# Weight differences of the second half: buffers of their own, stores one weight tile later, loads pinned behind weight loads

## The chip, the cores and the metric

The kernel runs on one core of one Trainium2 chip. The metric is the device time in microseconds (us) of one execution; lower is better. The core has TensorE (PE, matrix products), VectorE (DVE), ScalarE (ACT), GpSimd (POOL) and SyncE (SP). SP does no arithmetic here: it issues the transfers (DMAs) one after the other, in the order in which they stand in its queue. A transfer whose condition isn't met yet holds up all that stand behind it in that queue.

## The reference

One decoder block (DEPTH 1) on 512 tokens of 2048 channels in f32, with sixteen heads of 64 channels in attention and eight groups of 128 channels in spatial gating:

```python
mod = silu(c) @ w_ada + b_ada                       # shift, scale, gate
h = rms_norm(x, norm_g) * (1 + scale) + shift
z = h @ w_in                                        # 2048 -> 7184
u_a, v_a, g_a, q_b, k_b, v_b, g_b, f_b = split(z)
y_a = chunked_spatial_gating(gelu(u_a), gelu(v_a), ln_g, ln_b, w_s, b_s) * silu(g_a)
y_b = forgetting_attention(q_b, k_b, v_b, f_b, b_f) * silu(g_b)
y = concatenate([y_a, y_b]) @ w_out                 # 2048 -> 2048
out = rms_norm(x + gate * y, final_g)
```

forgetting_attention is causal softmax attention whose logits get the difference of two cumulated sums of log(sigmoid(f)) added. Group A mixes the tokens of each chunk of 128 by a lower triangular 128 x 128 matrix per group.

## The kernel before

**Products.** Every f32 operand is split into a rounded high part and the rest, its low part. A product is then three PE products: high by high, low by high, high by low (lines 145 to 147 in mm_cols, where weights are stationary; 154 to 156 in mm_toks, where the tokens are).

**Weight tiles.** w_tile (L117) brings a weight tile in: SP loads 512 KB (one weight tile) into a raw tile of the pool tag "raw" with four buffers (L123), ScalarE makes whi from it (L129), and VectorE (in some groups POOL) subtracts to make wlo (L130). A raw buffer is free again when that subtraction is done. The instructions of w_tile have a raised priority (WPRI), so a planner, which orders the instructions of each engine ahead of time by its own estimated timeline, puts them well ahead of the products that use them: the loads stand about four weight tiles ahead.

**Work between the tiles.** After the products of each weight tile the code calls tick(), which takes one entry from a list `slots` and one from a list `fillers`. `slots` holds the attention of the four groups of heads (u = 0 to 3), in eight entries each: scores, the softmax sums (lse), probabilities (probs) and values. `fillers` holds work that is independent of the products. The projection's column groups come in the order va, ga, v0, q0, k0, gb0, q1, k1, v1, gb2, q2, k2, v2, q3, k3, v3, gb1, gb3. The output projection follows, in two halves of 1024 columns: unit(0) and unit(1).

**The softmax sums.** lse takes the sums of a group of four heads, turns them with a PE transpose, splits them into a tile lt, and eight small DMAs on SP (L507) copy rows of lt into the tiles that hold q (the rows "q<-lt" of a profile). Only then can PE make the products t of probs (L523 and L524; the second reads those rows). After these come exponentials, splits, and the products of values.

**The weight differences.** The output projection makes each half with seven block products in place of eight. Four of the seven need differences of blocks of w_out: b12 - b11, b12 - b22, b22 - b11 and b21 - b22. They are made in advance and stored in DRAM (tsum, "ts" in the profile). For the first half this is done in eight steps (sum_step) while va is made. For the second half it is done in sixteen parts (sum_part, k = 0 to 7, p = 0 and 1; in the text part number 2k + p, counted from 0, in the profile ts_k_p). Each part is one filler: two loads of 256 KB (L640, L641) into a [128, 4, 256] tile of the tag "raw", the same four buffers as the weight tiles; four subtractions on POOL (L644); one store of 512 KB (L646). The store stands in SP's queue where the planner puts it, and whatever stands behind it waits until POOL's last subtraction is done.

**The gate.** The same list has 32 gate_steps, in which POOL builds the adaLN gate (L603, L604) from 512 KB loads in "raw", and four gate_sums. Before the change the order of the list is: gate_steps of all four column groups with gate_sum(0) to gate_sum(2) among them, then parts 0 to 2, gate_sum(3), and parts 3 to 15.

**wsp.** A [128, 8, 2, 128] tile holds the split matrices of spatial gating (8 KB per partition). It is last read by mix_head, early in the projection. Its pool buffer is used again by a tile "wide" in unit(1) alone.

Of the kernel before, what the change touches and what calls it, by code (L numbers as in the profile page):

```python
# [8 lines left out]
F32 = mybir.dt.float32  # L9
F32R = mybir.dt.float32r  # L10
# [5 lines left out]
P = 128  # L16
# [11 lines left out]
def trunk_kernel(  # L28
# [70 lines left out]
    newest = [None]  # L99
    newest_mm = [None]  # L100

    def load(dst, src, late=False):
        with ExitStack() as es:
            if queue:
                es.enter_context(tc.issue_after((newest[0] if late else queue[-1]).ins))
            newest[0] = nc.sync.dma_start(dst, src)
            if CHAIN[0]:
                queue.append(newest[0])

    hh = [None] * KB  # L110
# [6 lines left out]
    def w_tile(segs, k0, nk, src=win_r, name="", pri=WPRI, loeng=None):  # L117
        n = sum(w for _, w in segs)
        with tc.high_priority(offset=pri):
            raw = wp.tile([P, nk, n], F32, tag="raw", name=f"raw_{name}", bufs=4)  # L120
            o = 0
            for c0, w in segs:
                (load if pri == 0 else nc.sync.dma_start)(  # L123
                    raw[:, :, o : o + w], src[:, k0 : k0 + nk, c0 : c0 + w]
                )
                o += w
            hi = wp.tile([P, nk, n], F32R, tag="whi", name=f"whi_{name}")
            lo = wp.tile([P, nk, n], F32R, tag="wlo", name=f"wlo_{name}")
            nc.scalar.activation(hi, raw, AF.Copy)  # L129
            (loeng or nc.vector).tensor_tensor(lo, raw, hi.bitcast(F32), ALU.subtract)  # L130
        return hi, lo
# [294 lines left out]
    vs_ = []  # L426
    wsp = pb.tile([P, 8, 2, P], F32R, name="wsp", tag="wsp")
    OFF = [0, 512, 896, 1152]
# [184 lines left out]
    def sum_step(u, k):  # L613
# [18 lines left out]
        else:  # L632
            nc.sync.dma_start(tsum[u][k // 2][:, :, js], o)

    def sum_part(u, k, p):

        c = slice(p * 256, p * 256 + 256)
        a = wp.tile([P, 4, 256], F32, tag="raw", name=f"ts{u}_{k}_{p}", bufs=4)
        w = wout_r[:, :, u * 1024 : (u + 1) * 1024].rearrange("p k (s n) -> p k s n", s=2)
        nc.sync.dma_start(a[:, 0:2, :], w[:, 8 + k, :, c])  # L640
        nc.sync.dma_start(a[:, 2:4, :], w[:, k, :, c])  # L641
        b11, b12, b21, b22 = (a[:, z, :] for z in range(4))
        for dst, l, r in ((b11, b12, b11), (b12, b12, b22), (b22, b22, b11), (b21, b21, b22)):
            nc.gpsimd.tensor_tensor(dst, l, r, ALU.subtract)  # L644
        o = (k % 2) * 512 + p * 256
        nc.sync.dma_start(tsum[u][k // 2][:, :, o : o + 256], a)  # L646

# [11 lines left out]
    def spatial_weights():  # L659
# [10 lines left out]
        for i in range(2):  # L670
            wt = bank("x", f"wsT{i}")
            for j in range(4):
# [3 lines left out]
            split(  # L676
                wsp[:, 4 * i : 4 * i + 4, 0, :], wsp[:, 4 * i : 4 * i + 4, 1, :],
                wt32.rearrange("p (h t) -> p h t", t=P),
# [80 lines left out]
    def mix_head(h):  # L759
# [4 lines left out]
        b2 = bias2[:, h, :]  # L764
        w2 = wsp[:, h].rearrange("p a t -> p (a t)")
        for n in range(2):
# [31 lines left out]
    v_group(0)  # L798
    heads_tiles()
    for g in range(4):  # L800
        for i in range(8):
            fillers.append(lambda g=g, i=i: gate_step(g, i))
            if g and i == 2:
                fillers.append(lambda g=g: gate_sum(g - 1))
    parts = [lambda k=k, p=p: sum_part(1, k, p) for k in range(8) for p in range(2)]
    fillers.extend(parts[:3] + [lambda: gate_sum(3)] + parts[3:])
    qk_group(0)
# [155 lines left out]
    def unit(u):  # L963
# [35 lines left out]
        if u:  # L999
            wide = pb.tile([P, 4, 512], F32, name="wide", tag="wsp")  # L1000
            u2, u3 = [wide[:, t, :] for t in range(2)], [wide[:, 2 + t, :] for t in range(2)]
        else:
            u2, u3 = tiles("u2", "yb", 8), tiles("u3", "yb", 8)
# [124 lines left out]
```

## Time and profile before

| what | before |
|---|---|
| median of 3 runs | 913.16 us (911.5 to 913.87) |
| profiled execution, its own time | 910.78 us |
| span of the profiled execution | 909.1 us |
| granted TensorE clock, mean | 0.988 |
| PE busy | 880.1 us (97%) |
| VectorE, ScalarE, POOL busy | 603.9, 445.4, 405.9 us |
| DMA | 188.91 MB, 208 GB/s |
| POOL's subtractions of the parts (L644) | 64, 53.3 us busy |
| POOL's gate steps (L603, L604) | 60 + 60, 195.7 us busy |

A row of the profile names line, engine, operation and tiles as out<-in, then the time it was busy, and in brackets how long the engine stood idle ahead of it and what ended that. The span is divided into 40 slices, each digit the busy tenths of one. Durations and places come from the one profiled execution, whose own time is 910.78 us; the three timed runs lie between 911.5 and 913.87 us.

### The profile page before, as it was taken

To read this page: it belongs to the slowest core of one execution; us is meant where nothing else is said; L and a number is where in the kernel's file an instruction comes from. 1 tells how busy PE (TensorE), PEld (TensorE's weight loads), DVE (VectorE), ACT (ScalarE), POOL (GpSimd) and SP (SyncE) were. 2 spreads that over 40 slices of the span, in tenths; PEclk is the share of its full clock that TensorE was granted. 3 is DMA by queue.
4 is the path that set the end of the run, shared out by engine and by line. 5 is a ranking of instruction groups with operands and counts; after the bars stand their busy time and mean duration, and the time that the engine had idled before them with its cause. 6 is when DMAs were issued, how large, how long until landed. Compare 5 with 4: busy or idle time off the path is not lost.

```text
span 909.1 us, 12698 instructions
## 1 busy us (share of the span) xinstructions
PE 880.1 (97%) x4408; PEld 744.3 (82%) x4408; DVE 603.9 (66%) x998; ACT 445.4 (49%) x775; POOL 405.9 (45%) x322
## 2 busy tenths in 40 slices
PE   6999999999999999999999999989999999999995
PEld 4888888887878997777889888978898888888884
DVE  4778888374547857454886554535655679996687
ACT  5663323452313234455666544645556657655454
POOL 1356554513324259888988879334641000000001
PEclk8999999999999999999999999999999999999999
DMA  9999996349893264545545454657686236577575
GB/s 339 353 352 355 355 318 202 110 147 323 305 332 110 51 190 140 154 144 156 170 129 163 152 148 155 201 182 220 208 246 203 76 104 220 186 242 250 180 238 202
DMA packets 139713, 188.91 MB, mean 208 GB/s; under 512 B 9968, under 2 KB 103360, under 8 KB 139136
## 3 DMA queue, kind: packets, MB, share of 16 engines
q1 hardware_dynamic: 139216, 187.53, 64.6%
q8 instruction: 35, 0.57, 0.3%
q10 hardware_dynamic: 432, 0.57, 0.2%
q14 instruction: 30, 0.25, 0.1%
HBM read 166.90 MB, written 20.97 MB: 207 GB/s over the span
## 4 chain that ended last, share of the span: by engine, by line
PE 77%; DMA 10%; DVE 5%; POOL 3%; issue 2%; ACT 2%; SPq 0%; POOLq 0%; ACTq 0%; DVEq 0%
PE s L145 6%; PE s L147 6%; PE s L146 6%; PE va L156 3%; PE va L155 3%; PE va L154 3%; PE gb L145 3%; PE gb L146 3%; PE gb L147 3%; PE vb L154 3%; PE vb L156 3%; PE vb L155 3%; PE k L147 2%; PE k L146 2%; PE woZ L911 2%
## 5 line engine op out<-in xcount | busy, mean ns | idle before, releaser
L603 POOL TENSOR_SCALAR gate<-gate,sc 128x512 f32<-128x512 f32 x60 | 103.7, 1738 | 24.5 <-DMA gate<-in_w_ada_dram 11.9
L604 POOL TENSOR_TENSOR gate<-gate,gate 128x512 f32<-128x512 f32 x60 | 92.0, 1536 | 1.7
L130 POOL TENSOR_TENSOR wlo_st<-raw_st,whi_st 128x1024 fp32r<-128x1024 f32 (+3 forms) x36 | 68.4, 1904 | 54.1 <-ACT whi_st L129 52.9
L145 PE MATMUL s<-hh,whi_st 128*128 128x512 f32 x224 | 87.8, 395 | 1.5 <-ACT hh L267 1.5
L146 PE MATMUL s<-hl,whi_st 128*128 128x512 f32 x224 | 87.8, 392 | 0.0
L66 ACT ACTIVATE whi_p<-p 128x1024 fp32r<-128x1024 f32 x52 | 55.2, 1061 | 55.2 <-PE woZ L912 20.1
L644 POOL TENSOR_TENSOR ts<-ts 128x256 f32<-128x256 f32 x64 | 53.3, 837 | 62.8 <-DMA ts<-in_w_out_dram 43.8
L244 DVE SCALAR_TENSOR_TENSOR acc<-ada,sc,acc 128x512 f32<-128x512 f32 x98 | 73.9, 754 | 6.7 <-DMA ada<-in_w_ada_dram 4.0
L67 DVE TENSOR_TENSOR wlo_p<-p,whi_p 128x1024 fp32r<-128x1024 f32 x52 | 63.4, 1220 | 20.2 <-ACT whi_p L66 20.1
L147 PE MATMUL s<-hh,wlo_st 128*128 128x512 f32 x224 | 76.1, 393 | 0.0
L155 PE MATMUL vb<-whi_vb,hl 128*128 128x256 f32 (+1 forms) x256 | 72.6, 286 | 0.0
L154 PE MATMUL vb<-whi_vb,hh 128*128 128x256 f32 (+1 forms) x256 | 71.8, 284 | 0.0
L156 PE MATMUL vb<-wlo_vb,hh 128*128 128x256 f32 (+1 forms) x256 | 71.1, 286 | 0.0
L129 ACT ACTIVATE whi_st<-raw_st 128x1024 fp32r<-128x1024 f32 (+3 forms) x36 | 31.2, 870 | 66.7 <-PE s L146 38.8
L955 POOL TENSOR_TENSOR sfin<-sfin,nhalf 128x1 f32<-128x1 f32 x2 | 1.5, 749 | 137.4 <-DVE sfin L1047 137.4
L145 PE MATMUL q<-hh,whi_q 128*128 128x512 f32 x128 | 51.4, 401 | 1.2 <-ACT whi_q L129 1.2
L146 PE MATMUL q<-hl,whi_q 128*128 128x512 f32 x128 | 51.0, 398 | 0.0
L145 PE MATMUL gb<-hh,whi_gb 128*128 128x512 f32 x128 | 50.4, 393 | 0.5 <-ACT whi_gb L129 0.5
L145 PEld LDWEIGHTS s<-hh,whi_st 128*128 128x128 f32 x224 | 42.4, 190 | 10.3 <-ACT hh L267 1.6
L145 PE MATMUL k<-hh,whi_k 128*128 128x512 f32 x128 | 50.0, 391 | 0.7 <-ACT whi_k L129 0.7
L154 PE MATMUL va<-whi_va,hh 128*128 128x512 f32 x128 | 50.3, 393 | 0.0
L147 PE MATMUL q<-hh,wlo_q 128*128 128x512 f32 x128 | 50.2, 399 | 0.1
(309 smaller groups left out, 2506.3 us busy)
## 6 DMA issues: line engine op xcount, KB each, us to landing
ada<-in_w_ada_dram SPq DMA_DIRECT2D x128, 256.0 KB
gate<-in_w_ada_dram SPq DMA_DIRECT2D x32, 512.0 KB
p<-ts SPq DMA_DIRECT2D x32, 512.0 KB
p<-in_w_out_dram SPq DMA_DIRECT2D x24, 512.0 KB
raw_va<-in_w_in_dram SPq DMA_DIRECT2D x16, 512.0 KB
raw_q<-in_w_in_dram SPq DMA_DIRECT2D x16, 512.0 KB
raw_k<-in_w_in_dram SPq DMA_DIRECT2D x16, 512.0 KB
raw_gb<-in_w_in_dram SPq DMA_DIRECT2D x16, 512.0 KB
```

The source lines that it names most:

```text
L66: a = nc.scalar.activation(hi, src, AF.Copy)
L67: return a, (eng or nc.vector).tensor_tensor(lo, src, hi.bitcast(F32), ALU.subtract)
L130: (loeng or nc.vector).tensor_tensor(lo, raw, hi.bitcast(F32), ALU.subtract)
L145: nc.tensor.matmul(pt, hi[:, j, cs], hh[k], start=(k == first), stop=False)
L146: nc.tensor.matmul(pt, hi[:, j, cs], hl[k], start=False, stop=False)
L147: nc.tensor.matmul(pt, lo[:, j, cs], hh[k], start=False, stop=(k == last))
L154: nc.tensor.matmul(o, ah[k][:, tsl], hi[:, j, :], start=(k == first), stop=False)
L155: nc.tensor.matmul(o, al[k][:, tsl], hi[:, j, :], start=False, stop=False)
L156: nc.tensor.matmul(o, ah[k][:, tsl], lo[:, j, :], start=False, stop=(k == last))
L244: nc.vector.scalar_tensor_tensor(sb if kk == KB - 1 else a, ga[:, j], col, a, ALU.mult, ALU.add)
L603: nc.gpsimd.tensor_scalar(ga[:, j], ga[:, j], sc[:, kk : kk + 1], None, ALU.mult)
L604: nc.gpsimd.tensor_tensor(a, a, ga[:, j], ALU.add)
```

## The change

1. Parts take their buffers from the tag "wsp", with two buffers of 4 KB per partition, and no longer from "raw". So that the tag fits, wsp becomes two tiles (heads 0 to 3 and 4 to 7) and "wide" becomes two tiles.
2. The loads of a part are pinned (tc.issue_after) behind the newest weight load that has been issued when sum_part runs: the planner may not put them ahead of it.
3. The store of a part is no longer issued in sum_part. It is kept as a function in late_stores and issued at the start of the next sum_part, one filler and so one weight tile later; it is pinned behind the newest weight load of that time. A last filler issues the store of part 15.
4. The order of the fillers: all gate work first, then two empty entries, gate_sum(3), and the 16 parts.

Lines after L105 are moved by the change: L123 is L125 after it, L145 to L147 become L147 to L149, L507 is L509, L524 is L526, L640 and L641 are both L648, L646 is L656.

```diff
--- before.py
+++ after.py
@@ -98,6 +98,7 @@
 
     newest = [None]
     newest_mm = [None]
+    newest_w = [None]
 
     def load(dst, src, late=False):
         with ExitStack() as es:
@@ -106,6 +107,7 @@
             newest[0] = nc.sync.dma_start(dst, src)
             if CHAIN[0]:
                 queue.append(newest[0])
+        return newest[0]
 
     hh = [None] * KB
     hl = [None] * KB
@@ -120,7 +122,7 @@
             raw = wp.tile([P, nk, n], F32, tag="raw", name=f"raw_{name}", bufs=4)
             o = 0
             for c0, w in segs:
-                (load if pri == 0 else nc.sync.dma_start)(
+                newest_w[0] = (load if pri == 0 else nc.sync.dma_start)(
                     raw[:, :, o : o + w], src[:, k0 : k0 + nk, c0 : c0 + w]
                 )
                 o += w
@@ -424,7 +426,7 @@
 
     fsplit = pb.tile([16, 2, S], F32R, name="fsplit", tag="fs")
     vs_ = []
-    wsp = pb.tile([P, 8, 2, P], F32R, name="wsp", tag="wsp")
+    wsp = [pb.tile([P, 4, 2, P], F32R, name=f"wsp{i}", tag="wsp", bufs=2) for i in range(2)]
     OFF = [0, 512, 896, 1152]
     sgb = {}
 
@@ -632,18 +634,28 @@
         else:
             nc.sync.dma_start(tsum[u][k // 2][:, :, js], o)
 
+    late_stores = []
+
     def sum_part(u, k, p):
 
         c = slice(p * 256, p * 256 + 256)
-        a = wp.tile([P, 4, 256], F32, tag="raw", name=f"ts{u}_{k}_{p}", bufs=4)
+        while late_stores:
+            late_stores.pop(0)()
+        a = pb.tile([P, 4, 256], F32, tag="wsp", name=f"ts{u}_{k}_{p}", bufs=2)
         w = wout_r[:, :, u * 1024 : (u + 1) * 1024].rearrange("p k (s n) -> p k s n", s=2)
-        nc.sync.dma_start(a[:, 0:2, :], w[:, 8 + k, :, c])
-        nc.sync.dma_start(a[:, 2:4, :], w[:, k, :, c])
+        for z, row in ((0, 8 + k), (2, k)):
+            with tc.issue_after(newest_w[0].ins):
+                nc.sync.dma_start(a[:, z : z + 2, :], w[:, row, :, c])
         b11, b12, b21, b22 = (a[:, z, :] for z in range(4))
         for dst, l, r in ((b11, b12, b11), (b12, b12, b22), (b22, b22, b11), (b21, b21, b22)):
             nc.gpsimd.tensor_tensor(dst, l, r, ALU.subtract)
         o = (k % 2) * 512 + p * 256
-        nc.sync.dma_start(tsum[u][k // 2][:, :, o : o + 256], a)
+
+        def store():
+            with tc.issue_after(newest_w[0].ins):
+                nc.sync.dma_start(tsum[u][k // 2][:, :, o : o + 256], a)
+
+        late_stores.append(store)
 
     def gate_sum(g):
         gsl = slice(2 * D + g * 512, 2 * D + (g + 1) * 512)
@@ -674,7 +686,7 @@
             wt32 = pb.tile([P, 512], F32, name=f"wt32_{i}", tag="p", bufs=2)
             nc.scalar.activation(wt32, wt, AF.Copy)
             split(
-                wsp[:, 4 * i : 4 * i + 4, 0, :], wsp[:, 4 * i : 4 * i + 4, 1, :],
+                wsp[i][:, :, 0, :], wsp[i][:, :, 1, :],
                 wt32.rearrange("p (h t) -> p h t", t=P),
             )
             rp = bank("x", f"rsw{i}")
@@ -762,7 +774,7 @@
         js = slice(j * P, (j + 1) * P)
         mt = pb.tile([P, 512], F32, name=f"mt{h}", tag="p", bufs=2)
         b2 = bias2[:, h, :]
-        w2 = wsp[:, h].rearrange("p a t -> p (a t)")
+        w2 = wsp[h // 4][:, h % 4].rearrange("p a t -> p (a t)")
         for n in range(2):
             mx = bank("x", f"mix{h}_{n}")
             for i in range(2):
@@ -797,13 +809,24 @@
     vs_.append(pb.tile([P, NT, 4, P], F32R, name="vs", tag="vs"))
     v_group(0)
     heads_tiles()
+    gates = []
     for g in range(4):
         for i in range(8):
-            fillers.append(lambda g=g, i=i: gate_step(g, i))
+            gates.append(lambda g=g, i=i: gate_step(g, i))
             if g and i == 2:
-                fillers.append(lambda g=g: gate_sum(g - 1))
+                gates.append(lambda g=g: gate_sum(g - 1))
+    gates.extend([lambda: None] * 2 + [lambda: gate_sum(3)])
     parts = [lambda k=k, p=p: sum_part(1, k, p) for k in range(8) for p in range(2)]
-    fillers.extend(parts[:3] + [lambda: gate_sum(3)] + parts[3:])
+    n = 0
+    while gates or parts:
+        if gates:
+            fillers.append(gates.pop(0))
+        elif False:
+            fillers.append(lambda: None)
+        else:
+            fillers.append(parts.pop(0))
+        n += 1
+    fillers.append(lambda: [f() for f in late_stores])
     qk_group(0)
     g_group(0)
     for u in range(1, 4):
@@ -997,8 +1020,8 @@
         X = [bank("x", f"woX{u}_{t}") for t in range(2)]
         product(X, "S2", w_sum(3, "p6"), True)
         if u:
-            wide = pb.tile([P, 4, 512], F32, name="wide", tag="wsp")
-            u2, u3 = [wide[:, t, :] for t in range(2)], [wide[:, 2 + t, :] for t in range(2)]
+            wide = [pb.tile([P, 2, 512], F32, name=f"wide{t}", tag="wsp", bufs=2) for t in range(2)]
+            u2, u3 = [w[:, 0, :] for w in wide], [w[:, 1, :] for w in wide]
         else:
             u2, u3 = tiles("u2", "yb", 8), tiles("u3", "yb", 8)
         evac(lambda t: nc.vector.tensor_tensor(u2[t], X[t], c1[t], ALU.add))
```

How the order moves, at three places. The first is SP's queue around the first DMA that copies a row of lt into q for the second attention group (u = 1, first head); raw_q_4 and raw_q_8 are weight tiles of q2, ts_2_0 and ts_2_1 are parts 4 and 5. Before:

```order
L646 DMA ts_0_1850<-ts_1_1_5610 512x1x256
L640 DMA ts_2_0_5714<-in_w_out_dram 128x2x256
L641 DMA ts_2_0_5714<-in_w_out_dram 128x2x256
L123 DMA raw_q_4_5722<-in_w_in_dram 128x4x256
L646 DMA ts_1_1851<-ts_2_0_5714 512x1x256
L640 DMA ts_2_1_5799<-in_w_out_dram 128x2x256
L123 DMA raw_q_8_5807<-in_w_in_dram 128x4x256
L641 DMA ts_2_1_5799<-in_w_out_dram 128x2x256
L507 DMA q_1_3069<-lt_5506 1x4x128 x2
```

With the change, in the same queue up to the same DMA:

```order
L125 DMA raw_q_4_5706<-in_w_in_dram 128x4x256
L656 DMA ts_0_1851<-ts_1_0_5699 512x1x256
L648 DMA ts_1_1_5784<-in_w_out_dram 128x2x256 x2
L125 DMA raw_q_8_5791<-in_w_in_dram 128x4x256
L648 DMA ts_2_0_5870<-in_w_out_dram 128x2x256 x2
L656 DMA ts_0_1851<-ts_1_1_5784 512x1x256
L125 DMA raw_q_12_5877<-in_w_in_dram 128x4x256
L648 DMA ts_2_1_5921<-in_w_out_dram 128x2x256
L656 DMA ts_1_1852<-ts_2_0_5870 512x1x256
L648 DMA ts_2_1_5921<-in_w_out_dram 128x2x256
L125 DMA raw_k_0_5946<-in_w_in_dram 128x4x256
L509 DMA q_1_3070<-lt_5488 1x4x128 x2
```

In both the loads of part 5 and the store of part 4 stand ahead of that DMA; with the change the weight loads raw_q_12 and raw_k_0 have come ahead of it too. The store of part 4 is now behind raw_q_12, and the first load of part 5 ahead of that store.

The second is PE's queue around the first L524 products of the same group (q_0 and q_1 with the numbers 5634 and 5635, or 5618 and 5619, are the accumulation banks of q2, each step three products of 512 columns). Before:

```order
L146 MATMUL q_1_5635<-hl_527,whi_q_0_5638 128x512
L147 MATMUL q_1_5635<-hh_526,wlo_q_0_5639 128x512
L524 MATMUL t_0_5578<-q_1_3069,k_1_3077 128x512
L524 MATMUL t_1_5586<-q_1_3069,k_1_3077 128x384
L524 MATMUL t_2_5594<-q_1_3069,k_1_3077 128x256
L524 MATMUL t_3_5602<-q_1_3069,k_1_3077 128x128
L145 MATMUL q_1_5635<-hh_531,whi_q_0_5638 128x512
L146 MATMUL q_1_5635<-hl_532,whi_q_0_5638 128x512
L147 MATMUL q_1_5635<-hh_531,wlo_q_0_5639 128x512
L145 MATMUL q_0_5634<-hh_718,whi_q_4_5724 128x512
```

With the change:

```order
L147 MATMUL q_1_5619<-hh_531,whi_q_0_5622 128x512
L148 MATMUL q_1_5619<-hl_532,whi_q_0_5622 128x512
L149 MATMUL q_1_5619<-hh_531,wlo_q_0_5623 128x512
L147 MATMUL q_0_5618<-hh_718,whi_q_4_5708 128x512
L526 MATMUL t_0_5562<-q_1_3070,k_1_3078 128x512
L526 MATMUL t_1_5570<-q_1_3070,k_1_3078 128x384
L526 MATMUL t_2_5578<-q_1_3070,k_1_3078 128x256
L526 MATMUL t_3_5586<-q_1_3070,k_1_3078 128x128
L148 MATMUL q_0_5618<-hl_719,whi_q_4_5708 128x512
```

Before, 21 products of the first weight tile of q2 stand ahead of the four t products; with the change all 24 of it and one of the next tile do.

The third is SP's queue at the last two weight tiles of v2 (raw_vb_8 and raw_vb_12), with what each waits for in brackets: DMAHW lanes stand for DMAs that must have landed, Pool and DVE for instructions of these engines. Before:

```order
L646 DMA ts_3_1853<-ts_6_0_6234 512x1x256 [waits DMAHW2_49,DMAHW1_49,Pool_49]
L870 DMA fga<-in_final_g_dram 128x1024 [waits DMAHW5_49,DMAHW4_49]
L123 DMA raw_vb_8_6344<-in_w_in_dram 128x4x256 [waits DMAHW0_49]
L646 DMA ts_3_1853<-ts_6_1_6336 512x1x256 [waits DMAHW6_49,DMAHW7_49,DMAHW3_49,Pool_49]
L640 DMA ts_7_0_6413<-in_w_out_dram 128x2x256 [waits DVE_49]
L641 DMA ts_7_0_6413<-in_w_out_dram 128x2x256
L123 DMA raw_vb_12_6421<-in_w_in_dram 128x4x256 [waits DMAHW3_49]
```

With the change:

```order
L125 DMA raw_vb_8_6328<-in_w_in_dram 128x4x256 [waits DVE_49]
L656 DMA ts_2_1853<-ts_5_1_6321 512x1x256 [waits DMAHW5_49,DMAHW4_49,Pool_49]
L648 DMA ts_6_0_6398<-in_w_out_dram 128x2x256 [waits DMAHW6_49,DMAHW3_49]
L648 DMA ts_6_0_6398<-in_w_out_dram 128x2x256
L732 DMA q_1_3076<-fsplit 2x1x512 [waits PE_49]
L733 DMA k_1_3084<-fsplit 2x1x512
L893 DMA fga<-in_final_g_dram 128x1024 [waits DMAHW6_49,DMAHW7_49,DMAHW5_49,DMAHW0_49]
L125 DMA raw_vb_12_6405<-in_w_in_dram 128x4x256 [waits DVE_49]
```

Before, a weight load waits there for a DMA to land, the store of the part that had its buffer; with the change it waits for VectorE, and the load of a part waits for two DMAs.

## The prediction

> **What bounds the kernel now.** I read the page's head and slices first, then what TensorE (PE) waited for, then stretches of 10 us, and last the chain of waits inside the stretches that stood out.
>
> ```profile
> span 909.1 us, 12698 instructions
> PE 880.1 (97%) x4408; PEld 744.3 (82%) x4408; DVE 603.9 (66%) x998; ACT 445.4 (49%) x775; POOL 405.9 (45%) x322
> PE   6999999999999999999999999989999999999995
> PEclk8999999999999999999999999999999999999999
> ```
>
> PE is busy 97% of the span; of the 29.0 us that it is not, most lies in the first and the last slice, which the change doesn't touch. Between them one slice shows an 8. So whatever the change does to DMA queues and POOL counts only where PE stands still, or runs slowly. The next rows are PE's waits, and PE's busy time, the other engines, granted clock, DMA share and GB/s in three stretches.
>
> ```profile
> PE t L524 <- DMA q<-lt: 3.8, 1, 3.8
> ...
> PE s L484 <- ACT s L490: 1.2, 2, 1.0
> 610.00:620.00 10.00, 7.43 (x23) 6.09 (x24) 4.03 (x9) 4.25 (x9) 3.37 (x5) 0.66 0.50 147
> 620.00:630.00 10.00, 10.00 (x50) 8.46 (x49) 5.74 (x9) 4.70 (x9) 7.35 (x8) 1.00 0.63 209
> 680.00:690.00 10.00, 9.00 (x73) 8.71 (x73) 4.83 (x12) 7.14 (x19) 5.03 (x6) 1.00 0.66 219
> ```
>
> PE waits once for 3.8 us, and in that stretch the clock falls to 0.66; once more for 1.0 us near 682. The chain of waits from 600 to 618 (start, length, what; SPq is SyncE's queue, which issues the DMAs) says why:
>
> ```profile
> 600.42 0.75 POOL ts L644
> ...
> 602.86 0.75 POOL ts L644
> ...
> 603.62 3.18 DMA ts<-ts
> ...
> 606.82 0.37 SPq L640
> ...
> 607.75 0.51 SPq L641
> ...
> 608.30 0.71 SPq L507
> ...
> 609.05 3.39 DMA q<-lt
> ...
> 612.57 1.40 PE t L524 x4
> ```
>
> PE's first L524 product needs the rows of lt (the softmax sums) in q. They come by L507, and L507 stands in SP's queue behind the store of part 4 (L646, which waited for POOL's four subtractions) and behind the load of part 5 (L640), whose buffer is free only when that store has landed.
>
> **The sum, part by part.** *What the first stall costs.* PE's own rows (start, length, what):
>
> ```profile
> 608.36 0.40 PE L147 MATMUL q<-hh,wlo_q 128*128 128x512 f32 x1
> 612.57 1.40 PE L524 MATMUL t<-q,k 128*128 128x512 f32 x4 [3.82 <-DMA q<-lt]
> 613.78 0.73 PE L145 MATMUL q<-hh,whi_q 128*128 128x512 f32 x1
> ...
> 617.72 0.45 PE L145 MATMUL q<-hh,whi_q 128*128 128x512 f32 x1
> 618.01 0.39 PE L146 MATMUL q<-hl,whi_q 128*128 128x512 f32 x1
> 618.24 0.40 PE L147 MATMUL q<-hh,wlo_q 128*128 128x512 f32 x1
> ```
>
> At full clock a 512-column product starts every 0.23 us (618.01 to 618.24), whatever its shown length. The last one ahead of the stall began at 608.36, so its place ended at 608.59, and PE stood for 612.57 - 608.59 = 3.98 us. Then it ran slowly: from 612.57 to 618.01 it did the four L524 products (512 + 384 + 256 + 128 = 1280 columns, 0.58 us at full pace) and ten of 512 columns (2.30 us), that is 2.88 us of work in 5.44. That is 2.56 us more. The stall costs 3.98 + 2.56 = 6.54 us.
>
> [...]
>
> *What the second stall costs.* First the chain, then PE:
>
> ```profile
> 671.08 6.11 DMA ts<-ts
> ...
> 677.21 3.80 DMA raw_vb<-in_w_in_dram
> ...
> 682.05 0.45 ACT s L490 x2
> 681.27 0.28 PE L155 MATMUL vb<-whi_vb,hl 128*128 128x256 f32 x1
> 682.54 0.33 PE L484 MATMUL s<-k,q 128*128 128x128 f32 x1 [1.00 <-ACT s L490]
> ```
>
> The load of raw_vb_12 waited for a part's store, because both use the pool "raw". ScalarE waited for that load with its exponentials queued behind it, and PE for those. The place of PE's last product ends at 681.27 + 0.12, so 1.15 us are lost, at full clock. After the change the tile takes its buffer from another weight tile (its wait is on VectorE) and is issued four tiles ahead, so the whole 1.15 us go.
>
> *What SP no longer waits for.* In the stretch of the parts, 555 to 690 us:
>
> ```profile
> SPq L646 <- POOL ts L644: 26.1, 14, 5.1
> SPq L123 <- DMA ts<-ts: 22.1, 10, 3.4
> ```
>
> The weight loads' 22.1 us of waiting for stores end, since parts leave "raw". The stores' 26.1 us shrink, because each is issued a tile later. Neither is PE's time except in the two stalls.
>
> *Is L507 in time now?* It still stands behind a store's landing: the load of part 5 needs the buffer of part 3. I walk SP's new order in the clock of before, with these rows:
>
> ```profile
> 586.11 1.22 DVE L130 TENSOR_TENSOR wlo_vb<-raw_vb,whi_vb 128x1024 fp32r<-128x1024 f32 x1
> 612.73 0.73 POOL L644 TENSOR_TENSOR ts<-ts 128x256 f32<-128x256 f32 x1 [2.07 <-DMA ts<-in_w_out_dram]
> 600.42 3.18 POOL L644 TENSOR_TENSOR ts<-ts 128x256 f32<-128x256 f32 x4 [4.69 <-DVE vs L67]
> 581.78 0.53 SPq L646 DMA_DIRECT2D ts<-ts  x1
> 589.21 0.37 SPq L640 DMA_DIRECT2D ts<-in_w_out_dram  x1
> 657.15 3.60 DMA ts<-ts
> 630.04 5.66 DMA ts<-in_w_out_dram
> ```
>
> raw_q_4 is issued when wlo_vb_8 is done, 587.3. Part 2's store follows (its loads went out before), then part 3's loads, say until 589.6. A load's second half lands 4.98 us after issue (607.75 to 612.73): 594.6. POOL's four subtractions take 3.18: part 3's store goes out at 597.8. A store lands after 3.18 to 7.43 us (581.78 to 589.21, where L640 waited for it); I take 3.60, the middle of the four rows (3.18, 3.60, 6.11, 7.43) towards the low side, since the two long ones stood among other large transfers. So 601.4. Then SP issues part 5's first half, part 4's store, part 5's second half and raw_k_0: 0.37 + 0.53 + 0.51 and about 0.4, with gaps 2.0. L507 starts at 603.4; its rows landed 612.44 - 608.30 = 4.14 us after it, at 609.05 + 3.39 = 612.44. So: 607.5.
>
> PE comes to L524 later than before: 25 products of 512 columns stand ahead instead of 21, four more, 0.92 us, at 608.59 + 0.92 = 609.5. That is 2.0 us of slack. With the slowest store, 7.43, the rows land at 611.4 and PE waits 1.9; with a load of 5.66 as well, 2.6 us.
>
> [...]
>
> *The rest at nothing.* The DMAs, subtractions and products are the same in number. The parts begin later, behind weight tiles, but are read only by the second half's products. The price if POOL or SP falls behind is the slower rival's. The split of wsp and "wide" moves no row on PE; I bound it, and the planner's small reshuffles of products against softmax work, by the short waits that PE shows elsewhere, 1.0 us either way, and take zero.
>
> Sum: -6.54 - 1.15 = -7.7 us. The profiled execution took 910.78 us (909.1 span and 1.7 around it), 2.4 below the median shown, 913.16; on its own time that is 903.1, on the median 905.5.
>
> **Rivals.**
> (a) *L507 waits again, shorter.* For it: it still stands behind a store's landing, and two of four such rows are over 6 us. Against: 2.0 us of slack. A wait of up to 2.6 us leaves 7.7 - 2.6 = 5.1: 905.5 to 908.1. [...]
> (b) *The stall only moves.* If part 4's subtractions come behind part 3's late, SP stands at part 4's store as it stood at 603.62, and PE again waits about 4 us with the slow clock. Then only the second stall goes: 913.16 - 1.15 = 912.0. For it: POOL's work per part is unchanged, and two buffers have taken the place of up to four. Against: stores come a tile later, when POOL should be done.
> (c) *Slower: two buffers are too few.* One buffer's round is load 4.98, POOL 3.18, store 3.18 to 7.43, 11.3 to 15.6 us, and it has two weight tiles' time, as SP goes on only when the buffer is back.
>
> ```profile
> 622.70 1.05 ACT L129 ACTIVATE whi_q<-raw_q 128x1024 fp32r<-128x1024 f32 x1
> 643.17 1.06 ACT L129 ACTIVATE whi_k<-raw_k 128x1024 fp32r<-128x1024 f32 x1 [0.85 <-PE k L146]
> ```
>
> Three tiles in 20.5 us: 13.6 us for two. Weights are issued four tiles (27 us) ahead, less about 7 for landing and conversion: 20 us of cover. With 16 parts, 8 rounds per buffer, PE is reached from a round of 13.6 + 20 / 8 = 16.1 us on; at 18 it stands 8 x 1.9 = 15 us, less the 7.7 gained: 920. Against: the slowest rows make 15.6.
> (d) *The change doesn't do what it says:* the planner could put the stores back beside POOL's work. Its order shows them behind the next weight load, so that is out; no chance of its own.
>
> **The numbers.** Forecast, both stalls gone or under 1 us left: 0.55, 905.5, its own range 903.5 to 907. (a) with 1 us or more left: 0.25, 906.5 to 910.6. (b) 0.12, about 912. (c) 0.08, 914 to 920. A difference under 0.3% (2.7 us, about the spread of the three runs) can't be told from none, so faster is below 910.4: 0.55 + nearly all of (a), 0.79; same 0.13; slower 0.08. The range reaches from 903.0 (the unknown 1 us and the runs' spread) to 911.0, the end of (a); what is left out is (b) in good part and (c).
>
> **What would show it.** Right: PE's list of waits has no q<-lt of over 1 us, the stretch 610 to 620 shows PE 10.00 and clock 1.00, no raw_vb load waits for ts<-ts, and the 1.0 us of s L484 is gone. Wrong: a wait of PE for q<-lt of 3 us or more with a clock below 1 behind it (b); PE waiting for whi_k or whi_vb and SP's L648 waiting for ts<-ts by more than 3 us at most parts (c). A time under 902 would say that the parts hindered PE in a way that its list of waits doesn't show.

## The result, and the profile after

The changed kernel took 907.42 us (median of 22 runs, 903.45 to 917.54) against 914.09 us of the kernel before (22 runs, 911.5 to 925.45). The ratio is 0.9923, with a 95% interval of 0.9902 to 0.9944: 7.0 us faster (5.1 to 9.0), clear of the 0.3% that the prediction set as its bound. The ratio leaves out the runs of a slower state, over 1.5% above the fastest of the same kernel, and so is not the quotient of the two medians. The forecast was 905.5, range 903.0 to 911.0. It started from 913.16, the median of three runs; on 914.09 the same 7.7 us would have given 906.4.

One slip of numbering in the sections ahead: the group whose sums PE waited for is the third of four (u = 2, not u = 1), its copies fall into the fourth q group, to which the raw_q tiles shown belong, and raw_vb_8 and raw_vb_12 are tiles of the fourth v group (it is q3 and v3, not q2 and v2). Rows, tiles and times there are as they stand. From here on: third and fourth group.

The profiled execution took 906.88 us. The page's head and PE's slices, then PE's waits (total, times, longest) and two stretches of 10 us:

```profile
span 905.1 us, 12701 instructions
...
PE   6999999999999999999999999999999999999995
```

```profile
PE t L526 <- DMA q<-lt: 1.8, 2, 1.2
PE o L541 <- DVE ptl L67: 1.8, 2, 1.4
...
PE s L486 <- ACT s L492: 0.2, 1, 0.2
```

```profile
610.00:620.00 10.00, 8.89 (x43) 7.63 (x44) 5.57 (x13) 6.78 (x12) 3.87 (x5) 1.00 0.64 200
680.00:690.00 10.00, 10.00 (x75) 9.48 (x74) 5.49 (x13) 6.17 (x15) 3.76 (x4) 1.00 0.65 203
```

The slice with an 8 is a 9 now. The 3.8 us wait is two short ones, the stretch from 610 has its full clock, and the 1.0 us of s L484 (L486 now) is gone. PE's rows at the two waits that are left:

```profile
609.57 0.39 PE L147 MATMUL q<-hh,whi_q 128*128 128x512 f32 x1
611.11 0.82 PE L526 MATMUL t<-q,k 128*128 128x512 f32 x4 [1.15 <-DMA q<-lt]
...
693.48 0.39 PE L148 MATMUL gb<-hl,whi_gb 128*128 128x512 f32 x1
694.53 0.82 PE L526 MATMUL t<-q,k 128*128 128x512 f32 x4 [0.66 <-DMA q<-lt]
```

Reckoned as before (the last product's place ends 0.23 us after its start), PE stood for 611.11 - 609.80 = 1.31 us in the third group and 694.53 - 693.71 = 0.82 us in the fourth, where it had not waited before.

**A ledger that leaves the start out.** The span is a poor measure for single executions: they differ by up to 9 us before the first weight product (last section). So for each run I take, from PE's timeline, the start of the first product of the fourth q group and of the first product of the output projection. What lies between is the whole stretch in which the two stalls lay:

| profiled execution | fourth q group | output projection | stretch | PE's waits for q<-lt, third and fourth group |
|---|---|---|---|---|
| before | 603.53 | 747.10 | 143.57 | 3.98, none |
| changed | 604.03 | 741.98 | 137.95 | 1.31, 0.82 |

The stretch is 5.6 us shorter. In the single execution the span is only 4.0 us shorter, because other places differ: from the first product of the second k group to the next v group it took 29.7 us against 28.1 (that is where o L541 waited 1.4 us), and from the output projection on 153.6 against 152.5. Both lengths vary between executions of the experiments as well (27.5 to 31.2, and 152.5 to 153.7, leaving out the two runs in which the parts run among the gate steps), so they are not laid to the change. The 7.0 us of the ratio are 1.4 more than the stretch shows; that is inside the interval, and no run places it.

### The profile page after: what moved, and what is told of

Read it like the earlier page. It is cut to its first block, busy times and chain, and to the rows that moved or that the text cites. A ratio compares the mean times of both kernels' runs of the same rounds, so it can differ in the third digit from the quotient of the medians.

```text
span 905.1 us, 12701 instructions
## 1 busy us (share of the span) xinstructions
PE 878.8 (97%) x4408; PEld 742.5 (82%) x4408; DVE 602.2 (67%) x998; ACT 444.9 (49%) x775; POOL 413.2 (46%) x322
## 4 chain that ended last, share of the span: by engine, by line
PE 75%; DMA 8%; DVE 5%; POOL 5%; issue 3%; ACT 2%; SPq 1%; POOLq 0%; ACTq 0%; DVEq 0%
PE s L147 6%; PE s L149 6%; PE s L148 6%; PE va L158 3%; PE va L156 3%; PE va L157 3%; PE vb L156 3%; PE vb L157 3%; PE vb L158 3%; PE gb L149 2%; PE gb L148 2%; PE gb L147 2%; POOL gate L605 2%; PE q L148 2%; PE q L147 2%
## 5 line engine op out<-in xcount | busy, mean ns | idle before, releaser
L605 POOL TENSOR_SCALAR gate<-gate,sc 128x512 f32<-128x512 f32 x60 | 106.6, 1786 | 24.2 <-DMA gate<-in_w_ada_dram 11.8
L147 PE MATMUL s<-hh,whi_st 128*128 128x512 f32 x224 | 88.0, 397 | 1.4 <-ACT hh L269 1.4
L651 POOL TENSOR_TENSOR ts<-ts 128x256 f32<-128x256 f32 x64 | 57.3, 903 | 59.0 <-DMA ts<-in_w_out_dram 56.2
L149 PE MATMUL s<-hh,wlo_st 128*128 128x512 f32 x224 | 76.6, 395 | 0.0
L147 PE MATMUL q<-hh,whi_q 128*128 128x512 f32 x128 | 50.6, 395 | 1.2 <-ACT whi_q L131 1.2
L147 PEld LDWEIGHTS s<-hh,whi_st 128*128 128x128 f32 x224 | 42.6, 191 | 10.1 <-ACT hh L269 1.5
L147 PE MATMUL k<-hh,whi_k 128*128 128x512 f32 x128 | 50.2, 392 | 0.7 <-ACT whi_k L131 0.7
L147 PE MATMUL gb<-hh,whi_gb 128*128 128x512 f32 x128 | 50.4, 393 | 0.5 <-ACT whi_gb L131 0.5
L148 PEld LDWEIGHTS s<-hl,whi_st 128*128 128x128 f32 x224 | 42.7, 191 | 9.3 <-DVE hl L283 0.3
L148 PE MATMUL gb<-hl,whi_gb 128*128 128x512 f32 x128 | 50.2, 392 | 0.0
```

What stands on the lines that cost most here:

```text
L147: nc.tensor.matmul(pt, hi[:, j, cs], hh[k], start=(k == first), stop=False)
L148: nc.tensor.matmul(pt, hi[:, j, cs], hl[k], start=False, stop=False)
L149: nc.tensor.matmul(pt, lo[:, j, cs], hh[k], start=False, stop=(k == last))
L605: nc.gpsimd.tensor_scalar(ga[:, j], ga[:, j], sc[:, kk : kk + 1], None, ALU.mult)
```

## The experiments

The theory: what counts is which transfers stand ahead of the copies of the sums (q<-lt) in SP's queue, and how late those are. The main rival: the buffers, late stores and pins help by themselves, by taking waits out of the weight loads.

**One instruction moved, in the kernel before.**

```diff
-        nc.sync.dma_start(tsum[u][k // 2][:, :, o : o + 256], a)
+        with ExitStack() as es:
+            if (k, p) == (2, 0):
+                es.enter_context(tc.issue_after(last_lt[2].ins))
+            nc.sync.dma_start(tsum[u][k // 2][:, :, o : o + 256], a)
```

(last_lt[u] is the last copy of the sums of group u.)

> The kernel before with one instruction moved: the store of part 4 stands in SP's queue behind the eight copies of the softmax sums of the third group (L507), and the planner then puts the loads of part 5 on a free buffer. Theory (the queue is the cause): PE's wait for q<-lt of 3.8 us and the slow clock behind it go, 6.5 us or nearly, so about 0.993 of before (907.5 us on a before of 914); the stretch 610 to 620 shows PE 9.8 or more and clock 1.00; the wait of s L484 for ScalarE of about 1 us stays. Rival (the copies land late because the DMA engines are full, wherever they stand in the queue): the wait stays at 3 us or more and the time within 1 us of before.

Measured: 906.30 us against 914.34, ratio 0.9891 (0.9841 to 0.9941). SP's queue at the copies, and PE there (this execution runs 7.5 us later than the one of before, 611.02 against 603.53 at the fourth q group):

```profile
610.00 5.22 SPq L509 DMA_DIRECT2D q<-lt  x8
615.32 0.39 SPq L123 DMA_DIRECT2D raw_q<-in_w_in_dram  x1
615.81 1.26 SPq L651 DMA_DIRECT2D ts<-ts  x2
```

```profile
615.85 0.39 PE L147 MATMUL q<-hh,wlo_q 128*128 128x512 f32 x1
616.08 0.75 PE L526 MATMUL t<-q,k 128*128 128x512 f32 x4
```

The copies start at 610.00, which is 602.5 in the clock of before, where they started at 608.30. PE goes through without a wait. The stretch is 136.97 us, 6.60 less than before. The prediction gave the first stall 6.54 us, but not all of the 6.60 is its own: PE's wait in the second stall, which was expected to stay at about 1 us, shrank to 0.4 (no run shows why), so about 6.0 us are left for the first. The queue is the cause, and this one move is worth about as much as the whole change. The rival, full DMA engines, falls. The main rival falls for this stall as well: here the weight loads still wait 13.8 us for stores between 555 and 700 us, and the gain came all the same.

**The order of the fillers alone.**

```diff
-    fillers.extend(parts[:3] + [lambda: gate_sum(3)] + parts[3:])
+    fillers.extend([lambda: None] * 2 + [lambda: gate_sum(3)] + parts)
```

> The kernel before with only the order of the fillers changed (all gate work first, two empty entries, gate_sum(3), then the 16 parts); parts stay in the tag raw, stores are issued at once, nothing is pinned. The copies of the third group's sums then stand behind two loads of part 4 and a weight load, and no store of that part is ahead of them. Theory (the place in the queue is all): stall 1 goes by the order alone, stall 2 stays since raw_vb_12 still waits for a part's store: 914 - 6.5 = 907.5, ratio 0.993. Rival (own buffers and late stores are what helps): the wait for q<-lt stays above 2.5 us and the time is 912 or more.

Measured: 930.86 us, ratio 1.0144 (1.0083 to 1.0204), slower. The theory missed. The signs of its rival (a wait above 2.5 us, 912 or more) came, but most of the time was lost at a place that neither had named. PE's waits, and the chain of waits ahead of the fourth group's sums:

```profile
PE t L524 <- DMA q<-lt: 15.0, 2, 11.4
```

```profile
696.32 3.18 DMA ts<-ts
...
699.51 0.37 SPq L123
...
699.98 4.88 DMA ts<-ts
...
704.87 0.37 SPq L123
...
705.29 0.69 SPq L507
```

The third group still waits 3.69 us, since the order of products changed as well and PE reaches L524 after 10 products of that weight tile in place of 21. And now the last parts fall on the fourth group's sums: two weight loads (L123) stand ahead of the copies, and each waits for a store to land, as they share the tag raw. PE stands for 11.58 us. The theory holds as to the place; I had looked at the third group's copies alone.

**The own buffers alone.** The edit is the change of wsp, "wide" and the tile's tag (wp/raw/4 to pb/wsp/2), and nothing else.

> The kernel before with only the own buffers (tag wsp, two buffers; wsp and wide split); the old order of fillers, stores at once, no pins. Without pins the planner puts all parts far ahead, among the gate steps, and none is left near the third group's sums. Theory: no store stands ahead of those copies and no weight load waits for a store, so both stalls go, 914 - 7.7 = 906.3, ratio 0.992, like the whole change. Rival (parts among the gate steps delay POOL and SP there): PE gets new waits for whi_k or whi_vb or q<-lt between 410 and 600 us, and the time is 910 or more.

Measured: 954.51 us, ratio 1.0432 (1.0380 to 1.0484), slower. The stretch of the stalls is 135.81 us, 7.8 less than before, as the theory said. But from the first q group to the fourth the kernel takes 318.3 us in place of 267.6. PE's longest wait and a stretch of 50 us (columns as before), then the same stretch of the kernel before:

```profile
PE k L145 <- ACT whi_k L129: 15.7, 5, 4.0
...
450.00:500.00 50.00, 41.91 (x175) 33.18 (x174) 24.88 (x31) 18.36 (x33) 45.37 (x37) 0.90 0.52 163
```

```profile
450.00:500.00 50.00, 49.22 (x322) 44.88 (x322) 37.89 (x75) 30.54 (x73) 43.82 (x30) 1.00 0.51 153
```

With a tag of their own nothing holds the parts back, and the planner puts them among the gate steps, where POOL was busy for 43.82 of 50 us already. Weights come late, PE stands, and the clock falls to 0.90. It was the rival's mechanism, and far dearer than the 910 at which its range began.

**The change with one part taken back, four times.** The store at once:

```diff
-        late_stores.append(store)
+        store()
```

> The changed kernel with the store of a part issued in its own sum_part, pinned behind the newest weight load of that moment, in place of one filler later. The planner's order near the sums is then the same as in the changed kernel. Theory: the late store is worth nothing by itself: 907.4, within 1 us of the changed kernel, ratio to before 0.992 to 0.994. Rival (the late store is what frees SP's queue): SP's wait of the stores for POOL grows from 33.8 us and the time is 910 or more.

Measured: 909.96 us, ratio 0.9942 (0.9905 to 0.9978). PE's wait for q<-lt is 3.6 us again, with a slow clock behind it, and the stretch 142.14 us. SP's queue in this run, and then in the changed kernel:

```profile
589.61 0.52 SPq L656 DMA_DIRECT2D ts<-ts  x1
590.19 0.61 SPq L125 DMA_DIRECT2D raw_q<-in_w_in_dram  x1
...
601.40 0.52 SPq L656 DMA_DIRECT2D ts<-ts  x1
```

```profile
587.70 0.37 SPq L125 DMA_DIRECT2D raw_q<-in_w_in_dram  x1
590.82 0.52 SPq L656 DMA_DIRECT2D ts<-ts  x1
...
599.72 0.53 SPq L656 DMA_DIRECT2D ts<-ts  x1
```

The late store lets the next weight load go ahead of the store that waits for POOL. Without it the store of part 2 holds that weight load back, and then weight and part loads start closer together. The first load of part 3, issued at 590.86, landed only after 6.36 us (in the changed kernel POOL had it 4.2 us after its issue); that the loads beside it slowed it is likely, but not tested by itself. Counted from the start of the fourth q group (603.13 here, 604.03 in the changed kernel), part 3's store goes out 1.73 us ahead of it in place of 4.31, 2.6 us later. PE's standing grows by about that much, from 1.31 to 3.78 us, and loses the clock. SP's wait at the stores for POOL grew from 33.8 to 37.1 us, as the rival said. "Worth nothing" was wrong for the stretch (4.2 us more); as to the time, the two intervals overlap.

The parts in raw again:

```diff
-        a = pb.tile([P, 4, 256], F32, tag="wsp", name=f"ts{u}_{k}_{p}", bufs=2)
+        a = wp.tile([P, 4, 256], F32, tag="raw", name=f"ts{u}_{k}_{p}", bufs=4)
```

> The changed kernel with its parts in the tag raw again (order of the fillers, pins and late stores kept). Theory: the weight loads wait for stores again, and ahead of the fourth group's sums the load raw_gb3_0 waits for the landing of part 15's store, as in the kernel with the new order alone: PE waits for q<-lt some 11 us there, with the slow clock behind it, and the time is 920 to 932. Rival (late stores are enough, the own buffers only save memory traffic on raw): both waits stay under 2 us and the time is 907 to 909.

Measured: 926.08 us, ratio 1.0150 (1.0117 to 1.0183), stretch 156.58 us.

```profile
PE t L526 <- DMA q<-lt: 14.4, 2, 12.1
```

As the theory said: 12.2 us of standing in the fourth group, behind weight loads that wait for stores. The third group cost 2.45 us, and the second stall came back, longer: PE stood 3.41 us up to 690.35 for ScalarE, which had waited 4.96 us for a raw_vb load that was issued at 684.82, just after a store had landed (681.20 + 3.56 = 684.76). So the shared buffers are shown to be the cause of the second stall too. With the new order of the fillers the own buffers are indispensable.

The old order of the fillers:

```diff
-    gates.extend([lambda: None] * 2 + [lambda: gate_sum(3)])
     parts = [lambda k=k, p=p: sum_part(1, k, p) for k in range(8) for p in range(2)]
+    gates.extend(parts[:3] + [lambda: gate_sum(3)])
+    parts = parts[3:]
```

> The changed kernel with the old order of the fillers (three parts ahead of gate_sum(3)); own buffers, pins and late stores kept. Ahead of the third group's sums then stand the store of part 6, which waits for POOL, and the load of part 7, which waits for the landing of part 5's store. Theory (what counts is which of these stand ahead of the sums and how late they are): a wait for q<-lt of 1 to 4 us in the third group, none in the fourth, and 906 to 912. Rival (the order is the part that helps): the full wait of 3.8 us with the slow clock, and 912 or more.

Measured: 909.92 us, ratio 0.9952 (0.9912 to 0.9991), a wait of 3.64 us with the slow clock, stretch 142.51 us. SP's queue:

```profile
609.36 0.57 SPq L125 DMA_DIRECT2D raw_q<-in_w_in_dram  x1
614.71 0.52 SPq L656 DMA_DIRECT2D ts<-ts  x1
615.28 1.65 SPq L648 DMA_DIRECT2D ts<-in_w_out_dram  x2
617.03 5.21 SPq L509 DMA_DIRECT2D q<-lt  x8
```

SP stood from 609.93 to 614.71 at the store of part 6, with the copies behind it. Wait and time are in the theory's range, and the clock was lost as the rival said.

No pins: both tc.issue_after in sum_part taken out.

> The changed kernel without the pins (order, own buffers and late stores kept). The planner then puts the parts ahead among the gate steps, as with the own buffers alone. Theory (loads of weights and gate steps share four buffers and POOL with them): PE waits for whi_k, wlo_q and whi_gb between 350 and 600 us, 40 us in all as with the own buffers alone: 945 to 958. Rival (the new order and late stores keep the parts out of the way): under 912.

Measured: 955.27 us, ratio 1.0424 (1.0352 to 1.0496); the stretch 135.61 us, and 322.5 us from the first q group to the fourth: as with the buffers alone. Without pins the change costs 4%.

**A longer round of the two buffers** (in the text t2).

```diff
+        for _ in range(4):
+            nc.gpsimd.tensor_scalar(b21, b21, ones[:, 0:1], None, ALU.mult)
```

> The changed kernel with four more operations on POOL per part (the last block multiplied by ones four times), so that a part keeps its buffer longer. The result is the same. POOL's time per part grows from 3.2 to about 6 to 7 us, and one round of a buffer from 11.3 to 15.6 us to some 15 to 19. Theory (PE is reached from a round of 16 us on): the planner spreads the parts further, SP's waits for POOL grow to over 45 us, and the time is 907 to 913. Rival (the weight loads have cover for it): within 1 us of the changed kernel. Third possibility (the parts run into the fourth group's sums as before): a wait for q<-lt over 4 us and 915 or more.

Measured: 920.19 us, ratio 1.0074 (1.0054 to 1.0093), the third possibility. PE's waits, and the chain ahead of the fourth group's sums:

```profile
PE t L526 <- DMA q<-lt: 9.7, 2, 6.8
...
PE k L147 <- ACT whi_k L131: 0.7, 1, 0.7
```

```profile
697.94 3.54 DMA ts<-ts
...
701.50 0.37 SPq L648
...
702.42 0.69 SPq L509
703.21 1.84 DMA q<-lt
```

POOL's work per part grew to 7.8 us (125.3 us for 16 parts), and the loads into one buffer follow each other 18.9 us apart (569.16 to 701.50, seven rounds). The weight loads have cover: PE waits for whi_k no longer than before (0.7 us). The later parts run into the fourth group's copies, behind a part's load that waits for a store.

**Can the rest be had?** The changed kernel once more, then with part 4's store and part 5's loads pinned behind the third group's copies (in the text t1), and then with two weight loads pinned behind the copies as well (t3):

```diff
+                if (k, p) == (2, 1):
+                    es.enter_context(tc.issue_after(last_lt[2].ins))
...
+                    if name in ("k3_0", "gb3_0"):
+                        es.enter_context(tc.issue_after(last_lt[2 if name == "k3_0" else 3].ins))
```

(The first two lines stand at the loads of a part, and the same two with (2, 0) at its store; the last two, in t3 alone, at the load in w_tile.)

> The changed kernel once more, as it is, to stand beside the next three on the same chip: 0.992 of before, and in its trace PE's waits for q<-lt of 1.3 us (third group) and 0.8 us (fourth group) again, at a clock of 1.00.

> The changed kernel with the store of part 4 and the loads of part 5 pinned behind the copies of the third group's sums as well. Theory (what is left of stall 1 is the load of part 5 that waits for the store of part 3): the wait of 1.3 us for q<-lt in the third group goes, the 0.8 us of the fourth stays: 1.3 us under the changed kernel, about 906. Rival (the later parts 4 and 5 push the next ones back and hold up something else): a new wait of 1 us or more after 615 us, and the time the same or longer.

> As t1_sums_first, and two weight loads (raw_k of the fourth q and k group, first tile; raw_gb of the last group, first tile) are pinned behind the copies of the third and the fourth group's sums, since each waited in the queue ahead of them for VectorE. Theory: PE's two waits for q<-lt (0.8 and 1.1 us in t1_sums_first) fall under 0.4 us each, 1 to 1.5 us less than t1_sums_first, some 2 us under the changed kernel, ratio to before about 0.990. Rival (what is left is the way of the sums themselves, or the two loads then come late): the waits stay, or PE waits for whi_k or whi_gb, and the time is that of the changed kernel.

| run | median us | ratio to before (95%) | stretch | waits for q<-lt, third and fourth group |
|---|---|---|---|---|
| changed, again | 905.61 | 0.9923 (0.9908 to 0.9937) | 138.18 | 0.77, 1.55 |
| t1 | 905.48 | 0.9905 (0.9873 to 0.9938) | 137.65 | 0.79, 1.07 |
| t3 | 906.66 | 0.9929 (0.9889 to 0.9969) | 135.63 | none, none |

The same kernel's waits vary between executions (1.31 and 0.82 in one, 0.77 and 1.55 in the other). t1 moves nothing that can be told, though its theory had the third group's wait gone: the copies then stand behind raw_k, which waits 1.0 us for VectorE, and wait another 1.0 us themselves for VectorE and ScalarE. t3 takes both waits away and has the shortest stretch of all kernels that have the parts in it (the two without, whose parts run earlier, have 135.61 and 135.81), 2.3 to 2.6 us under the changed kernel. Its 12 runs fall into two groups, 903.0 to 907.5 and 911.3 to 915.1, and its ratio can't be told from that of the changed kernel. So no version is shown to beat it.

## Why the prediction was right, and where it was off

**Stall 1: right in cause, price and place.** The price of 6.54 us, read from PE's rows, came out as 6.0 to 6.6 when one moved instruction took the stall away; the upper figure holds some of the second stall. The change itself leaves 1.31 us of standing there.

**Stall 2: right.** 1.15 us were forecast to go; s L486 waits 0.2 us in all, and the stretch 680 to 690 is 10.00. With the parts back in raw it returned, at 3.41 us.

**"L507 is in time": wrong, and the largest miss.** PE came when forecast (609.80; forecast 609.5). The rows landed at 607.66 + 3.31 = 610.97, not at 607.5. The steps, from the changed kernel's SP queue:

```profile
603.35 0.37 SPq L648 DMA_DIRECT2D ts<-in_w_out_dram  x1
603.94 0.53 SPq L656 DMA_DIRECT2D ts<-ts  x1
604.51 1.79 SPq L648 DMA_DIRECT2D ts<-in_w_out_dram  x1
...
606.90 5.23 SPq L509 DMA_DIRECT2D q<-lt  x8
```

```profile
586.91 3.88 POOL L651 TENSOR_TENSOR ts<-ts 128x256 f32<-128x256 f32 x4 [5.47 <-DMA ts<-in_w_out_dram]
...
597.31 2.38 POOL L651 TENSOR_TENSOR ts<-ts 128x256 f32<-128x256 f32 x3 [1.02 <-DMA ts<-in_w_out_dram]
```

| step | forecast | measured | what differed |
|---|---|---|---|
| raw_q_4 issued | 587.3 | 587.70 | |
| part 3's loads out | 589.6 | 593.05 | SP stood at part 2's store until 590.82: POOL had got that part only at 586.91 |
| part 3's store | 597.8 | 599.72 | |
| part 5's first load, its buffer back | 601.4 | 603.35 | 3.63 us after the store; 3.60 was taken |
| copies issued | 603.4 | 606.90 | 3.55 us for four issues, not 2.0: one load's issue took 1.79, not 0.51 |
| rows in q | 607.5 | 610.97 | |

Two sizes failed: part 2's subtractions were taken as done when SP came to its store, and an issue as half a microsecond each time. The bound beside it ("PE waits 1.9; with a load of 5.66 as well, 2.6") was large enough for both, but by luck: it was built from a slow store and a slow load, and the store of part 3 landed as forecast. The sign named for "right", no wait for q<-lt over 1 us and PE at 10.00 from 610 to 620, did not come; the rows show 1.2 us and 8.89. With 2.1 us left in two waits, what happened is case (a), a left-over wait at full clock with 905.5 to 908.1, rather than the likeliest case of under 1 us left. The time of 907.4 says the same.

**The fourth group was not looked at.** Its 0.82 us have no place in the sum. It is also where the new order alone, the parts in raw and t2 stood for 7 to 12 us. The walk was made for the place where the stall had been, and not for the next place of the same form.

**"The stores' 26.1 us shrink": wrong, and part of the wait that was left.** SP waited longer at the stores, for POOL (33.8 us in place of 26.1) and for the loads of parts (10.9 in place of 6.4):

```profile
SPq L656 <- POOL ts L651: 33.8, 13, 5.2
...
SPq L656 <- DMA ts<-in_w_out_dram: 10.9, 8, 3.2
```

POOL waits longer for its loads: of its idle time ahead of the subtractions a part's load ended 56.2 us, in place of 43.8. That the pins behind weight loads are the reason is likely and was not tested alone. It reached PE at part 2's store, in the table above. What changed is who stands behind the stores. The weight loads' 22.1 us of waiting for stores are gone, as forecast.

**The rest at nothing: right as far as the stretch shows.** 143.57 - 137.95 = 5.62 us; by the terms it is 6.54 + 1.15 - 1.31 - 0.82 = 5.56. The two edits with no price, wsp and "wide", show none.

**The rivals.** (b), part 4 late behind part 3, did not come, but it was close: POOL ended part 4 at 603.92, and SP came to its store just then (603.94). Two of the four runs with one part taken back had the outcome of (b), 3.6 to 3.8 us of standing with the slow clock, at 910 us: the old order by its mechanism, SP standing at a store that waits for POOL, and the store at once by a late store of part 3. (c) forecast 920 for a round of 18 us by late weights; t2, with a round of 18.9 us, took 920.19 by another way, the fourth group's sums, while the weights stayed in time. So (c)'s mechanism is not borne out, and that the two times agree is chance.

**The clock.** The 905.5 to 908.1 of (a) count a left-over wait at full clock, and the 1.31 and 0.82 us that were left kept it (granted clock 1.00 from 611 to 620 and from 694 to 700). In the kernel before, 3.98 us of standing were followed by (617.72 - 613.78) / 9 = 0.44 us per product in place of 0.23, and 1.15 us by a granted clock of 1.00 (682 to 690). What happens between these two lengths the profile of before does not show, and in the experiments waits of 1.60 to 3.09 us lost the clock (last section): (a) with the slow clock was not ruled out. The 910.6 at which its range ends is 908.1 with the 2.56 us of the first stall's slow clock on top; no run shows a left-over wait of 2.6 us with that price. What the runs showed in its place is the price of longer waits, and it was near: with 3.64 to 3.78 us of standing, some 3 us more were lost (store at once: 142.14 less t3's 135.63 less the wait of 3.78: 2.7; old order: 3.2), for which the forecast had 2.56.

**The way of the copies: right.** The forecast took 4.14 us from the issue of the copies to the first copy's rows in q, as before. In the trace they are there 610.97 - 606.90 = 4.07 us after issue: no delay by the store of part 4, which stands ahead of them, shows. It is a weak test, as that store had gone out 2.96 us ahead of the copies.

## What to carry to other kernels

A small transfer on which the critical engine waits should be followed in its queue from each place where it is issued, not only where it stalls today: everything ahead of it that waited for another engine or for a landing was part of its latency here (before: the store of part 4 went out at 603.62, when POOL was done, the load behind its landing at 606.82, the copies at 608.30). The four parts of this change hold each other up: the buffers alone cost 4.3%, the new order alone 1.4%, the change without the pins 4.2%, without the buffers 1.5%, and one move of one store gave about what all four together gave. Where executions differ by several microseconds at the start, measure the stretch between two events of the same engine instead of the span.

## What the runs showed of the hardware that was not expected

**Waits of 1.60 to 3.09 us cost the clock, once 1.2 us late; their length alone does not decide.** In t2, PE's timeline at the third group:

```profile
608.78 0.39 PE L147 MATMUL q<-hh,whi_q 128*128 128x512 f32 x1
612.10 0.82 PE L526 MATMUL t<-q,k 128*128 128x512 f32 x4 [2.93 <-DMA q<-lt]
...
613.27 0.50 PE L147 MATMUL q<-hh,whi_q 128*128 128x512 f32 x1
613.57 0.63 PE L148 MATMUL q<-hl,whi_q 128*128 128x512 f32 x1
...
616.56 0.52 PE L149 MATMUL q<-hh,wlo_q 128*128 128x512 f32 x1
```

PE stood 3.09 us, ran 1.2 us at full pace, then some 3.3 us at 0.43 us per product, then at full pace again. In the kept traces every stand of 3.54 us or more after 200 us of the span (up to 12.23) was followed by slow products at once, some 0.43 us each in place of 0.23. Below that both outcomes occur. In the run with the parts in raw, stands of 2.45 and 3.41 us (ending at 618.07 and 690.35) kept the full clock. With the buffers alone, 2.77 us ending at 379.67 lost it, 1.77 us later and after one more stand of 0.74 us; without the pins, 2.17 us ending at 385.66 lost it at once. And in t3 much shorter ones lost it:

```profile
456.65 0.39 PE L546 MATMUL o<-ptl,vs 128*128 128x256 f32 x1 [1.43 <-DVE ptl L67]
...
458.60 0.63 PE L152 MATMUL k<-hh,whi_k 128*128 128x512 f32 x1
```

PE stood 1.60 us there and, one product later, 0.61 us; from 458 to 461 its granted clock is 0.50. The changed kernel has the same two stands at the same place (ending at 456.76 and 457.49), and from 458 to 461 its granted clock is 1.00. So one pair of stands had two outcomes, and one drop came 1.2 us late. Stands of 1.60, 2.17, 2.77 and 3.09 us lost the clock, stands of 2.45 and 3.41 us kept it; what decides between them is not shown.

**The start differs by 6 to 9 us.** In 9 of the 13 profiled executions the first weight product (s L145, or its line after an edit) started at 30.3 to 33.1 us, in the other four at 39.2. The stretch from 20 to 40 us, of the old-order run (late start) and of the kernel before:

```profile
20.00:40.00 20.00, 18.58 (x89) 18.40 (x88) 7.65 (x15) 8.86 (x17) 2.22 (x2) 0.50 1.09 352
```

```profile
20.00:40.00 20.00, 18.46 (x118) 16.35 (x119) 15.77 (x25) 12.34 (x24) 5.82 (x5) 0.91 1.09 352
```

The transfers move the same 352 GB/s; PE's granted clock is 0.50 over the stretch with the late start, and 0.91 in the kernel before. Which of the two, the lower clock or the late start, causes the other is not shown. The start is the likely source of the two groups of times in t3: the mean granted clock is 0.976 to 0.979 in its longer runs and 0.985 to 0.991 in the others, and 0.978 in the profiled executions of t1 and of the run with one instruction moved, which started late. It was not tested by itself. What follows is hardly longer for it: from the first to the fourth q group three of the four runs with the late start took 267.4 to 267.5 us and the one with the parts in raw 268.4, the kernel before 267.6.
